# Two-layer hybrid decoder trunk: wide products of two weight parts for both blocks, then the narrow ones, in runs of sixteen

## The chip, the cores and the metric

The kernel runs on one NeuronCore of a Trainium2 chip. The time is device time of one execution, in microseconds (us). Several runs were timed, and one further execution was profiled; the profile gives the start and length of every instruction on each engine: TensorE (PE, with the weight load PEld apart), VectorE (DVE), ScalarE (ACT), GpSimd (POOL), and SyncE (SP), which here only issues transfers.

## The reference

A sequence of 256 positions with 2048 features goes through two layers, each of which adds its branch to the stream, and a last RMSNorm. Both branches project the normalised input, attend, multiply by a SiLU gate and project back. Cut to what matters:

```python
for i in range(2):
    h = rmsnorm(x, norm_g[i])
    if i == 0:      # forgetting attention, 32 heads of 64
        q, k, v, gate, f = split(h @ fox_w_in[0])          # 4 x 2048 + 32 columns
        c = cumsum(log_sigmoid(f + fox_b_f[0]))            # per head
        y = softmax(q k^T / 8 + c[t] - c[s], causal) v
        x = x + (y * silu(gate)) @ fox_w_out[0]
    else:           # window of 128, 32 query heads on 4 key heads, sinks
        q, k, v, gate = split(h @ swa_w_in[0])             # 2 x 2048 + 2 x 256 columns
        q, k = partial_rope(q), partial_rope(k)
        y = softmax(q k^T / 8, band, with sink) v
        x = x + (y * silu(gate)) @ swa_w_out[0]
return rmsnorm(x, final_g)
```

## The kernel before

**Products.** Every projection is cut into units of 256 output columns (`Unit`), and each unit's 2048 input features into parts, four of 512 in most units (a part is four tiles of 128 features). Values are float32, multiplied in two halves: `load` brings a part from memory (a transfer that SP issues into one of four buffers `wraw`), ACT rounds it (L222, the high half) and DVE subtracts (L223, the low half), both into one of five buffers `w` (`WBUFS`). The activations, `xs` and `ys`, lie split in the same way. `block(u, p, c)` issues the products of part `p` of unit `u` for one block `c` of 128 output rows (0 or 1). It has two steps: **wide** products, in which the high half of the stationary tile meets both halves of the moving one (512 columns), and **narrow** ones, in which its low half meets the high half (256 columns). For a part of four tiles these are four wide and four narrow products. `block` issues the wide ones and returns `narrow`, which issues the narrow ones and, after a unit's last part, calls its consumer (`done`). A unit accumulates in two PSUM banks, of which there are two pairs (`acc`). Units with `halves=False` (the values of layer 0, two groups at a time, and the last output unit) don't divide in this way.

**The stream.** `stream` is the list of all (unit, part) in order: layer 0 by groups of four heads (`fox_units`: queries, keys, for odd groups the values of two, gate), its output units (`first_out`, whose first three are interleaved by part), layer 1 (`swa_units`: keys, values, then for each of eight groups queries and gate), and its output units (`last_out`). The loop at the end walks it. At each part it first asks for the part three further on (`fetch`, L1019), issues block 0 of this part and then block 1 of the part before, so that block 1 runs one part late. For units in `quiet` (layer 0 from its third group on, output units from the fourth on) the narrow products of block 0 come after the whole of block 1: wide 4, wide 4, narrow 4, narrow 4, runs of eight. For all others, layer 1 among them, they follow at once: runs of four.

**What sets the order around it.** TensorE's instructions keep the order in which they are written. All else of the attention hangs on a clock of ticks: a tick passes after every two products of a `halves` unit, eight in a part, 32 in a unit, and `after(n, fn)` runs `fn` n ticks later. When a unit's keys (layer 0) or queries (layer 1) are complete, their consumer sets the group's events by a table: scores of the first and second pair of heads (`ps_s`), transposes (`pt`, `pt_w`), product with the values (`psy`). In layer 0 (`FOX_DUE`) the scores are due 18 and 50 ticks after the keys, in layer 1 (`SWA_DUE`) 31 and 49 after the queries. On ACT and DVE the order is the program's, as the scheduler of the build leaves it: casts and subtractions of weights stand in one queue with copies out of PSUM (L295), exponentials (L337), scalings (L356, L359) and the steps below.

**Lines that the steps touch.** Keys of layer 0: L295 copies half of the accumulators, L577 adds the other, L578 scales, and L582, L583 (ACT) and L585, L586 (DVE) write the split keys `kk`. Queries of layer 1: L295, L838 add, L840 shuffle, L843, L844 rotary products, L876 sum, L369 (ACT) and L370 (DVE) the split queries. Softmax of layer 1: scores and bias L453, L392, L457, maxima L887 to L890, exponentials L337, L893, L357, L353, scalings L356 and L359, transposes `pt_w`, copies L475 and L477. Gate: L324, L325, L312 to L319.

Of the kernel before, what the change touches and what calls it, by code (L numbers as in the profile page):

```python
# [49 lines left out]
WBUFS = 5  # L50
# [7 lines left out]
def trunk(  # L58
# [19 lines left out]
    def mm(*args, **kw):  # L78
        tc.keep_in_program_order(nc.tensor.matmul(*args, **kw))  # L79
# [28 lines left out]
    def tick():  # L108
        clock[0] += 1
        for fn in due.pop(clock[0], ()):  # L110
            with tc.high_priority(HP):
                fn()
# [99 lines left out]
    def load(unit, p):  # L212
        src, off, _, _, s = unit.parts[p]
        n = unit.n
        ask(unit, p, nc.sync)
        raw = unit.raw[:, off : off + s, :]
        w = wpool.tile([P, 2048], F32R, tag="w", name="w")
        w = w[:, 0 : 2 * s * n].rearrange("p (k h n) -> p k h n", h=2, n=n)
        high, low = w[:, :, 0, :], w[:, :, 1, :]
        if isinstance(src, tuple):  # L220
            high, low = (a.rearrange("p k (g n) -> p k g n", g=2) for a in (high, low))
        state["split"] = nc.scalar.copy(high, raw)  # L222
        nc.vector.tensor_tensor(out=low, in0=raw, in1=high.bitcast(F32), op=ALU.subtract)  # L223
        loaded[unit, p] = w

    def block(unit, p, c):
        _, _, _, kt0, s = unit.parts[p]
        w, a = loaded[unit, p], unit.acts
        if p == 0 and (c == 0 or unit.apart):

            pool, tag, banks = unit.apart if c == 1 else (*unit.acc, 2)
            ps = pool.tile([P, banks, 512], F32, tag=tag, name="acc")
            if unit.apart:
                unit.ps[c] = ps[:, 0, :]
            else:
                unit.ps, unit.both = [ps[:, i, :] for i in range(2)], ps
        n = unit.n if unit.kind == "tok" else S
        both, ps = unit.ps[c], unit.ps[c][:, 0:n]
        cs = slice(c * P, (c + 1) * P)
        def operands(i):  # L240

            kt = kt0 + i
            if unit.kind == "tok":
                return a[:, kt, 0, cs], a[:, kt, 1, cs], w[:, i]
            return w[:, i, 0, cs], w[:, i, 1, cs], a[:, kt]

        first, last = kt0 == 0, kt0 + s == KT
        ops = [operands(i) for i in range(s)]
        def done():
            if p < len(unit.parts) - 1:  # L250
                return
            if unit.apart:
                unit.consume(c, both)
            elif c == 1 and unit.kind == "tok":
                for i in range(2):
                    unit.consume(i, unit.ps[i])
            elif c == 1:
                unit.consume(unit.both)

        def narrow():  # L260
            for i, (_, sl, mv) in enumerate(ops):
                mm(ps, sl, mv[:, 0, :], start=False, stop=last and i == s - 1)
                if i % 2:
                    tick()
            done()

        if unit.halves:

            for i, (sh, _, mv) in enumerate(ops):
                mm(both, sh, mv.rearrange("p h n -> p (h n)"), start=first and i == 0, stop=False)  # L270
                if i % 2:
                    tick()
            if s % 2:
                tick()
            return narrow
        if n == 512:
            for i, (sh, sl, mv) in enumerate(ops):
                mm(ps, sh, mv[:, 0, :], start=first and i == 0, stop=False)
                mm(ps, sh, mv[:, 1, :], start=False, stop=False)
                tick()  # L280
                mm(ps, sl, mv[:, 0, :], start=False, stop=last and i == s - 1)
                tick()
        else:
            for i, (sh, sl, mv) in enumerate(ops):
                mm(ps, sh, mv[:, 0, :], start=first and i == 0, stop=False)
                mm(ps, sl, mv[:, 0, :], start=False, stop=False)
            for i, (sh, _, mv) in enumerate(ops):
                mm(ps, sh, mv[:, 1, :], start=False, stop=last and i == s - 1)
                tick()
        done()  # L290
        return lambda: None
# [13 lines left out]
    def whole(src, kind, consume, **kw):  # L305
        return Unit(quarters(src), kind, consume, **kw)
# [351 lines left out]
    groups = [FoxGroup(g) for g in range(8)]  # L658
# [36 lines left out]
    def out_units(src, done):  # L695
        def consumer(u):
            def consume(ps):
                x = xT[:, 2 * u : 2 * u + 2, :]
                nc.vector.tensor_add(x, low_half(ps), x)  # L699
                nc.vector.tensor_add(x, ps[:, :, 0:S], x)  # L700
                for c in range(2):
                    done(2 * u + c)

            return consume

        first = [
            whole(src[u], "wgt", consumer(u), acts=ys, acc=(ps_s, "S") if u == 2 else None)
            for u in range(3)
        ]
        return first + [whole(src[u], "wgt", consumer(u), acts=ys) for u in range(3, 8)]  # L710
# [115 lines left out]
    fox_units = units  # L826
    first_out = out_units(fox_out_d, to_layer1)
# [80 lines left out]
    swa_units = [whole(swa_in_d[8], "wgt", swa_k), whole(swa_in_d[9], "tok", swa_v)]  # L908
# [6 lines left out]
    last_out = out_units(swa_out_d, to_end)  # L915
# [56 lines left out]
    def fetch(upto):  # L972
        while fetched[0] < min(upto, len(stream)):
            load(*stream[fetched[0]])
            fetched[0] += 1
# [37 lines left out]
    state["sink"] = sink  # L1013

    quiet = set(fox_units[fox_units.index(groups[2].units[0]):] + first_out[3:] + last_out[3:7])
    prev = None
    for i, (u, p) in enumerate(stream):  # L1019
        fetch(i + 1 + LOOK)  # L1020
        if u is last_out[7]:
            if p == 0:
                block(*prev, 1)()
            block(u, p, 0)()
            continue
        narrow = block(u, p, 0)
        if u not in quiet:
            narrow()
        if prev is not None:
            block(*prev, 1)()  # L1030
        if u in quiet:
            narrow()
        prev = (u, p)
    for p in range(len(last_out[7].parts)):
        block(last_out[7], p, 1)()
# [65 lines left out]
```

## Time and profile before

| | us |
|---|---|
| median of 3 runs (825.01 to 825.56) | 825.55 |
| the profiled execution | 824.71 |
| its span, first to last instruction | 823.0 |
| mean granted TensorE clock | 0.996 |
| transfers, mean | 183 GB/s |

The page has the busy time of each engine (with the share of the span and the number of instructions), the chain of work that ended last, the costliest groups of instructions, and the transfers. Views of the trace list waits, groups and instructions by time. In rows of the timeline stand start, length, engine, line, operation, what it writes and reads, and how many; in brackets the idle time ahead of it and what ended it. Matmuls are pipelined and are recorded for longer than they hold the engine, so two starts tell more of them than a length.

### The profile page before, as it was taken

The numbers are of one execution on the slowest core, as the hardware profiler recorded it, in microseconds if no ns is written. First come the engines' busy times: TensorE is split into PE (matmuls) and PEld (weight loads), VectorE is DVE, ScalarE is ACT, GpSimd is POOL, SyncE is SP. The second block draws the span as 40 slices with busy tenths as digits, with TensorE's granted clock in tenths as the row PEclk, the third lists the DMA queues.
The fourth block names the chain that finished last, engine by engine and source line by source line (L and its number), as shares of the span: only waits on it lengthen the run. The fifth ranks groups of instructions, "written<-read, shape, count | busy, mean of one in ns | idle before, by whom it ended". The sixth has DMA issues, their size and how long they took to land.

```text
span 823.0 us, 13160 instructions
## 1 busy us (share of the span) xinstructions
PE 812.7 (99%) x4746; PEld 706.5 (86%) x4746; DVE 643.8 (78%) x1171; ACT 527.2 (64%) x978; POOL 63.5 (8%) x96
## 2 busy tenths in 40 slices
PE   8999999999999999999999999999999999999996
PEld 7988888888888888888888888888888888888885
DVE  6988866987678876788749668689999899976654
ACT  7776665665657566575647546577678776875551
POOL 1012010000101010010003110000000000001210
PEclk9999999999999999999999999999999999999998
DMA  9766656655656466655555565555455554464642
GB/s 294 252 213 225 195 186 199 198 176 178 208 167 218 153 195 202 192 196 162 175 181 187 187 203 162 187 165 180 141 164 161 175 170 139 154 195 146 206 126 102
DMA packets 47264, 150.49 MB, mean 183 GB/s; under 512 B 5552, under 2 KB 7248, under 8 KB 47200
## 3 DMA queue, kind: packets, MB, share of 16 engines
q1 hardware_dynamic: 44640, 141.84, 54.8%
q0 software_dynamic: 1408, 6.36, 2.3%
q10 hardware_dynamic: 1152, 1.47, 0.5%
q8 instruction: 37, 0.61, 0.3%
q14 instruction: 27, 0.22, 0.1%
HBM read 147.50 MB, written 2.15 MB: 182 GB/s over the span
## 4 chain that ended last, share of the span: by engine, by line
PE 98%; DMA 0%; DVE 0%; ACT 0%; DVEq 0%; issue 0%; SPq 0%
PE acc L79 90%; PE ps_s L79 3%; PE psy L79 3%; PE pt L82 1%; PE pt_w L82 1%; DMA wraw<-in_vf_dram 0%; DVE scaled L813 0%; PE ps_n L79 0%; PE rows L79 0%; DVEq L1095 0%; ACT w L222 0%; DVE tail_x L784 0%; PE pt_r L82 0%; DVE rest L788 0%; SPq L930 0%
## 5 line engine op out<-in xcount | busy, mean ns | idle before, releaser
L79 PE MATMUL acc<-xs,w 128*128 128x512 f32 (+1 forms) x2624 | 480.3, 339 | 0.0
L79 PEld LDWEIGHTS acc<-xs,w 128*128 128x128 f32 x2624 | 406.2, 189 | 56.7 <-issue 1.3
L223 DVE TENSOR_TENSOR w<-wraw,w 128x1024 fp32r<-128x1024 f32 (+4 forms) x277 | 324.8, 1178 | 92.2 <-ACT w L222 90.7
L222 ACT CAST w<-wraw 128x1024 fp32r<-128x1024 f32 (+4 forms) x277 | 277.7, 1009 | 125.1 <-PE acc L79 93.9
L79 PE MATMUL acc<-ys,w 128*128 128x256 f32 (+1 forms) x960 | 170.5, 338 | 0.0
L79 PEld LDWEIGHTS acc<-ys,w 128*128 128x128 f32 x960 | 147.8, 189 | 21.0 <-issue 0.6
L79 PE MATMUL acc<-w,xs 128*128 128x512 f32 (+2 forms) x512 | 111.9, 363 | 1.4 <-ACT w L222 1.3
L79 PEld LDWEIGHTS acc<-w,xs 128*128 128x128 f32 x512 | 86.0, 188 | 15.3 <-ACT w L222 1.5
L295 ACT COPY half<-acc 128x512 f32<-128x512 f32 x56 | 32.8, 586 | 78.7 <-PE acc L79 78.4
L337 ACT ACTIVATE st<-st,mx 128x128 f32<-128x128 f32 (+1 forms) x128 | 56.6, 443 | 2.1 <-DVE mx L641 2.1
L720 POOL TENSOR_TENSOR acc<-acc,sq 128x256 f32<-128x256 f32 x28 | 24.4, 871 | 88.1 <-ACT sq L714 87.0
L79 PE MATMUL ps_s<-kk,q 128*128 128x256 f32 (+1 forms) x160 | 30.4, 304 | 0.0
L392 DVE CUSTOM_DVE_ANT_0 st<-ps_s,st 128x128 f32<-128x128 f32 (+1 forms) x96 | 28.2, 332 | 0.9
L123 POOL TENSOR_SCALAR_AFFINE_SELECT bc<-bc 128x256 f32<-128x256 f32 x32 | 23.7, 759 | 64.2 <-DMA bc<-negc_d 64.2
L79 PEld LDWEIGHTS ps_s<-kk,q 128*128 128x128 f32 x160 | 24.5, 188 | 2.9 <-issue 0.2
L718 POOL COPY acc<-sq 128x256 f32<-128x256 f32 x2 | 1.4, 676 | 326.1 <-ACT sq L714 326.1
L519 ACT CAST ys<-gt 128x512 fp32r<-128x512 f32 x16 | 9.9, 619 | 25.1 <-DVE gt L518 25.1
L426 ACT COPY pts<-pt 128x384 f32<-128x384 f32 x32 | 15.3, 478 | 16.2 <-PE pt L82 16.2
L628 POOL DMA_DIRECT2D bc<-negc_d x16 | 8.9, 555 | 217.3 <-DVE mx L392 192.3
L337 ACT ACTIVATION_READ_ACCUMULATOR st<-st,mx 128x1 f32 x128 | 23.9, 187 | 0.0
L157 DVE SCALAR_TENSOR_TENSOR xs<-xT,g_sb,xs 128x256 fp32r<-128x256 f32 x32 | 20.6, 679 | 2.9 <-ACT xs L156 2.9
L699 DVE TENSOR_TENSOR xT<-half,xT 128x512 f32<-128x512 f32 x15 | 11.4, 758 | 12.3 <-ACT half L295 12.3
(146 smaller groups left out, 594.0 us busy)
## 6 DMA issues: line engine op xcount, KB each, us to landing
wraw<-in_fox_in_dram SPq DMA_DIRECT2D x96, 512.0 KB, 4.4
wraw<-in_swa_in_dram SPq DMA_DIRECT2D x72, 512.0 KB, 4.2
wraw<-in_fox_out_dram SPq DMA_DIRECT2D x32, 512.0 KB, 4.4
wraw<-in_swa_out_dram SPq DMA_DIRECT2D x32, 512.0 KB, 4.3
wraw<-in_fox_in_dram SPq DMA_DIRECT2D x54, 256.0 KB, 3.7
bc<-negc_d POOLq DMA_DIRECT2D x16, 384.0 KB, 4.7
wraw<-in_vf_dram SPq DMA_DIRECT2D x4, 288.0 KB, 4.7
xT<-in_xt_dram SPq DMA_DIRECT2D x2, 512.0 KB, 7.9
```

The lines of the kernel that those rows point to most:

```text
L79: tc.keep_in_program_order(nc.tensor.matmul(*args, **kw))
L82: tc.keep_in_program_order(nc.tensor.transpose(out, in_, ident))
L123: return nc.gpsimd.affine_select(out=ap, in_=ap, compare_op=ALU.is_ge, fill=NEG, base=base, pattern=pattern, channel_multiplier=mult,)
L157: nc.vector.scalar_tensor_tensor(out=xs[:, kt, 1, :], in0=xT[:, kt, :], scalar=g, in1=xs[:, kt, 0, :].bitcast(F32), op0=ALU.mult, op1=ALU. ...
L222: state["split"] = nc.scalar.copy(high, raw)
L223: nc.vector.tensor_tensor(out=low, in0=raw, in1=high.bitcast(F32), op=ALU.subtract)
L295: nc.scalar.copy(s, ps[:, :, S : 2 * S])
L337: nc.scalar.activation(st[:, hh, rng], st[:, hh, rng], AF.Exp, bias=nm[:, qb, hh : hh + 1], accum_out=l[:, qb, hh : hh + 1],)
L392: nc.vector.tensor_tensor_reduce(out=st, in0=high, in1=st, scale=self.scale, scalar=LOWEST, op0=ALU.add, op1=ALU.max, accum_out=self.mx[:, ...
L426: nc.scalar.copy(group.new_pts(self.j, hh)[:, hh, self.j, :], pt[:, 0 : 3 * P])
L699: nc.vector.tensor_add(x, low_half(ps), x)
L720: nc.gpsimd.tensor_add(sums[0], sums[0], s)
```

## The change

The set `quiet` becomes `paired` and takes in the units of layer 1. Units in it that divide into wide and narrow go through a path of their own: at an even part the next five parts are asked for, then the wide products of both blocks are issued, and their narrow ones are held; at the odd part the wide products of both blocks follow, and then all narrow ones: wide 16, narrow 16. The next part is asked for once the even part's narrow products are issued. Block 1 no longer runs a part late there, and a unit's consumer comes at the unit's own end. All other units keep the order of before.

```diff
-    quiet = set(fox_units[fox_units.index(groups[2].units[0]):] + first_out[3:] + last_out[3:7])
-    prev = None
+    paired = fox_units[fox_units.index(groups[2].units[0]):] + first_out[3:] + last_out[3:7]
+    paired += swa_units
+    paired = {u for u in paired if u.halves}
+    prev, held = None, []
     for i, (u, p) in enumerate(stream):
+        if u in paired:
+            if p % 2 == 0:
+                if prev is not None:
+                    block(*prev, 1)()
+                    prev = None
+                fetch(i + WBUFS)
+            held += [block(u, p, c) for c in range(2)]
+            if p % 2:
+                for k, narrow in enumerate(held):
+                    narrow()
+                    if k == 1:
+                        fetch(i + WBUFS)
+                held = []
+            continue
         fetch(i + 1 + LOOK)
         if u is last_out[7]:
-            if p == 0:
+            if p == 0 and prev is not None:
                 block(*prev, 1)()
             block(u, p, 0)()
             continue
-        narrow = block(u, p, 0)
-        if u not in quiet:
-            narrow()
+        block(u, p, 0)()
         if prev is not None:
             block(*prev, 1)()
-        if u in quiet:
-            narrow()
         prev = (u, p)
```

Counted over TensorE's whole order, a narrow product is followed by a wide one 364 times before and 196 times now. The number of products is the same.

**DVE, keys of layer 0, group 6** (groups 2 and 4 alike). `w` is a subtraction of weights. Before:

```order
L223 TENSOR_TENSOR w<-wraw,w 128x4x256 x3
L577 TENSOR_TENSOR k<-acc,half 128x512
L578 TENSOR_TENSOR k<-k,r_n_497 128x512
L223 TENSOR_TENSOR w<-wraw,w 128x4x256
L585 TENSOR_TENSOR kk<-k,kk 64x2x256
```

Now:

```order
L223 TENSOR_TENSOR w<-wraw,w 128x4x256 x3
L577 TENSOR_TENSOR k<-acc,half 128x512
L223 TENSOR_TENSOR w<-wraw,w 128x4x256
L578 TENSOR_TENSOR k<-k,r_n_497 128x512
L585 TENSOR_TENSOR kk<-k,kk 64x2x256
```

A subtraction moved ahead of L578, and the last of the three ahead of L577 is of a part whose buffer comes free only at the eighth narrow product of the keys' last pair.

**ACT, layer 1, the end of a group's second pair of heads.** `es` is the sinks' exponential, `pts` the transposed weights, `half` the copy of the next group's queries. Before:

```order
L891 ACTIVATE es<-es 128x4
L337 ACTIVATE st,l<-st,mx 128x128
L337 ACTIVATE st,l<-st,mx 128x256
L475 COPY pts<-pt_w 128x2x128
L295 COPY half<-acc 128x512
L356 ACTIVATE st<-st,rl 128x128 x2
L359 ACTIVATE st<-st,rl 128x128 x2
L222 CAST w<-wraw 128x4x256 x2
```

Now:

```order
L891 ACTIVATE es<-es 128x4
L337 ACTIVATE st,l<-st,mx 128x128
L337 ACTIVATE st,l<-st,mx 128x256
L222 CAST w<-wraw 128x4x256
L356 ACTIVATE st<-st,rl 128x128 x2
L359 ACTIVATE st<-st,rl 128x128 x2
L295 COPY half<-acc 128x512
L222 CAST w<-wraw 128x4x256 x2
```

The copy of the queries stands behind a cast and the four scalings.

**DVE, layer 1, the queries that follow.** `rot_t` and `rot` are the rotated queries. Before:

```order
L838 TENSOR_TENSOR rot_t<-acc,half 128x512
L840 STREAM_SHUFFLE rot<-rot_t 128x512
L843 TENSOR_TENSOR rot_t<-rot_t,rope_c 128x512
L844 TENSOR_TENSOR rot<-rot,rope_c 128x512
L223 TENSOR_TENSOR w<-wraw,w 128x4x256
L477 TENSOR_TENSOR pts<-pt_w,apart 128x2x256
L876 TENSOR_TENSOR rot_t<-rot_t,rot 128x512
L223 TENSOR_TENSOR w<-wraw,w 128x4x256
L370 TENSOR_TENSOR q_5495<-rot_t,q_5495 64x2x256 x2
```

Now:

```order
L838 TENSOR_TENSOR rot_t<-acc,half 128x512
L840 STREAM_SHUFFLE rot<-rot_t 128x512
L223 TENSOR_TENSOR w<-wraw,w 128x4x256
L477 TENSOR_TENSOR pts<-pt_w,apart 128x2x256
L843 TENSOR_TENSOR rot_t<-rot_t,rope_c 128x512
L844 TENSOR_TENSOR rot<-rot,rope_c 128x512
L223 TENSOR_TENSOR w<-wraw,w 128x4x256
L876 TENSOR_TENSOR rot_t<-rot_t,rot 128x512
L223 TENSOR_TENSOR w<-wraw,w 128x4x256
L370 TENSOR_TENSOR q_5486<-rot_t,q_5486 64x2x256 x2
```

Three subtractions instead of two lie between the sum L838 and the split queries.

## The prediction

> **What bounds the kernel now.** I read the page's busy line and its chain first, then the windows by stage.
>
> ```profile
> PE 812.7 (99%) x4746; PEld 706.5 (86%) x4746; DVE 643.8 (78%) x1171; ACT 527.2 (64%) x978; POOL 63.5 (8%) x96
> PE 98%; DMA 0%; DVE 0%; ACT 0%; DVEq 0%; issue 0%; SPq 0%
> L79 PE MATMUL acc<-xs,w 128*128 128x256 f32 x1312 | 206.9, 283 | 0.0
> 498.00:745.00 247.00, 247.00 (x1464) 213.25 (x1464) 213.62 (x462) 175.36 (x385) 0.00 (x0) 1.00 0.53 167
> wraw<-in_swa_in_dram SPq DMA_DIRECT2D x72, 512.0 KB, 4.2
> ```
>
> 98% of the chain that ends last is TensorE, so the time is the sum of what its products take; nothing else delays it. But the fourth row, the stretch of layer 1's input products (columns: stretch, length, then busy PE, PE weight load, DVE, ACT, POOL, clock), has DVE busy for 213.62 of 247 us and ACT for 175.36. Both are close behind, and in the trace both work through their instructions in the program's order. (The third row is used below: a narrow product is recorded for 0.28 us, so its result is there 0.16 after the next one may start.) Two numbers matter therefore: what TensorE saves by the regrouping, and whether the two queues still deliver the operands of the score products in time.
>
> **What the longer runs save.** Two rows of the chain cover 182 products each; the four after them, of the timeline, are runs of one width alone.
>
> ```profile
> 213.07 31.44 PE acc L79 x182
> 505.82 31.97 PE acc L79 x182
> 284.64 3.56 PE L79 MATMUL acc<-w,xs 128*128 128x512 f32 x15
> 288.04 0.40 PE L79 MATMUL ps_s<-kk,q 128*128 128x256 f32 x2
> 802.10 5.92 PE L79 MATMUL acc<-w,ys 128*128 128x256 f32 x48
> 807.86 0.50 PE L79 MATMUL ps_cols<-ones,acc 128*128 128x1 f32 x4
> ```
>
> From start to start, a wide product in a long run takes (288.04 - 284.64) / 15 = 0.2267 us and a narrow one (807.86 - 802.10) / 48 = 0.1200. The first chain row lies where runs are of eight: by the program's order it holds 88 wide and 94 narrow products, 19.95 + 11.28 = 31.23 us at those rates, so 0.21 us remain for 11 returns from narrow to wide, **0.019 us each**. The second, in runs of four, holds 92 and 90: 31.66 us, and 0.31 remain for some 22 returns, 0.014 each. The change takes 28 units from four returns to two (28 x 2 x 0.019 = 1.06 us), and 18 units of layer 1 from eight to two (18 x (8 x 0.014 - 2 x 0.019) = 1.33). That is **2.4 us less**. No trace here has runs of sixteen: if a return there cost nothing, the saving would be 28 x 4 x 0.019 + 18 x 8 x 0.014 = 4.1; if it cost twice as much, 4.1 - 92 x 0.038 = 0.6. I take the cost of a run of eight, the nearest row. The number of products, of ticks and of loads does not change.
>
> [...]
>
> **Loads.** A wide run now uses two parts, so a buffer of split weights comes free after 8 of the 16 narrow products and the next at their end, about 0.95 and then 4.6 us apart instead of every 2.8. SP issues the same transfers, whose landing (4.2 us, row above) stays ahead because the raw tiles have four buffers; each part is still asked for two pairs, some 8 to 11 us, before its first product, and needs two passes of 1.05 and 1.2 us. I cost this at nothing for TensorE. Its effect is on the queues: a cast that waits for such a buffer holds what stands behind it on ACT.
>
> **Layer 0, the keys of groups 2, 4 and 6.** These rows are of group 6; DVE first, then ACT, then PE.
>
> ```profile
> 334.25 1.22 DVE L223 TENSOR_TENSOR w<-wraw,w 128x1024 fp32r<-128x1024 f32 x1 [1.57 <-ACT w L222]
> 336.53 0.69 DVE L577 TENSOR_TENSOR k<-acc,half 128x512 f32<-128x512 f32 x1 [1.06 <-ACT half L295]
> 337.25 0.69 DVE L578 TENSOR_TENSOR k<-k,r_n 128x512 f32<-128x512 f32 x1
> 339.00 0.68 DVE L585 TENSOR_TENSOR kk<-k,kk 64x512 fp32r<-64x512 f32 x1
> 341.11 0.69 DVE L586 TENSOR_TENSOR kk<-k,kk 64x512 fp32r<-64x512 f32 x1
> 335.91 0.59 ACT L295 COPY half<-acc 128x512 f32<-128x512 f32 x1 [1.70 <-PE acc L79]
> 337.98 0.62 ACT L582 CAST kk<-k 64x512 fp32r<-64x512 f32 x1 [0.54 <-DVE k L578]
> 341.77 0.63 PE L79 MATMUL ps_s<-kk,q 128*128 128x512 f32 x2
> ```
>
> The last key half is ready at 341.11 + 0.69 = 341.80 and the second score product starts at about 342.0: 0.2 us to spare, on a chain of 5.9 us from the end of the unit at 335.9. In the new order the end of the unit moves to its own sixteenth narrow product, and TensorE comes to the scores after a whole pair (16 x 0.2267 + 0.02 = 3.65, and 16 x 0.12 = 1.92, together 5.57) and four wide products (0.93): the second score product is due 6.73 after the unit's last issue. The keys, with the same zero: a weight subtraction (1.22) now stands ahead of L577 and starts only at 0.33, since its cast waited for the eighth narrow product and DVE for the cast; L577 ends at 2.16; another 1.15 of subtraction now stands between L577 and L578, which ends at 3.90; the cast L582 and the four alternating passes L585, L586 take 3.5 as now (337.94 to 341.80 is 3.86, less a subtraction's hold of the first); end 7.4. **TensorE waits 7.4 - 6.7 = 0.7 us, three times: 2.1.** Bounds 0.4 to 1.0 each, by half a subtraction either way.
>
> **Layer 1, the queries of every odd group.** ACT, then DVE, then PE, around an even group's second pair and the next group's queries.
>
> ```profile
> 594.06 1.05 ACT L222 CAST w<-wraw 128x1024 fp32r<-128x1024 f32 x1 [1.32 <-issue]
> 595.01 0.40 ACT L337 ACTIVATE st<-st,mx 128x128 f32<-128x128 f32 x1
> 596.88 0.62 ACT L312 ACTIVATE gate_e<-gt 128x512 f32<-128x512 f32 x1
> 602.17 0.39 ACT L337 ACTIVATE st<-st,mx 128x128 f32<-128x128 f32 x1
> 604.09 0.35 ACT L475 COPY pts<-pt_w 128x256 f32<-128x256 f32 x1
> 604.34 0.58 ACT L295 COPY half<-acc 128x512 f32<-128x512 f32 x1
> 604.89 0.70 ACT L356 ACTIVATE st<-st,rl 128x128 f32<-128x128 f32 x2
> 606.08 1.04 ACT L222 CAST w<-wraw 128x1024 fp32r<-128x1024 f32 x1
> 600.83 0.69 DVE L315 SCALAR_TENSOR_TENSOR gate_e<-gt,gate_e 128x512 f32<-128x512 f32 x1
> 605.29 0.68 DVE L838 TENSOR_TENSOR rot_t<-acc,half 128x512 f32<-128x512 f32 x1
> 606.79 0.69 DVE L843 TENSOR_TENSOR rot_t<-rot_t,rope_c 128x512 f32<-128x512 f32 x1
> 608.00 1.22 DVE L223 TENSOR_TENSOR w<-wraw,w 128x1024 fp32r<-128x1024 f32 x1
> 609.14 0.68 DVE L477 TENSOR_TENSOR pts<-pt_w,apart 128x512 f32<-128x512 f32 x1
> 609.74 0.68 DVE L876 TENSOR_TENSOR rot_t<-rot_t,rot 128x512 f32<-128x512 f32 x1
> 611.58 1.40 DVE L370 TENSOR_TENSOR q<-rot_t,q 64x512 fp32r<-64x512 f32 x2
> 607.58 0.60 PE L82 MATMUL pt_w<-ident,st 128*128 128x128 f32 x4
> 607.93 7.01 PE L79 MATMUL acc<-xs,w 128*128 128x512 f32 x38
> 614.78 0.88 PE L79 MATMUL ps_s<-kk,q 128*128 128x256 f32 x6
> ```
>
> Now the queries are ready at 612.98 and the scores start at 614.78: 1.8 us to spare. In the new order, from the end of an even group's first score products (zero): a cast ahead of the first exponentials waits for the eighth narrow product of the next pair, 0.24 + 3.65 + 0.95 + 0.16 = 5.0, and takes 1.05. The exponentials (1.87, 595.01 to 596.88) end near 8.0. DVE then does the sums of the first pair (0.6), the rest of the second pair's reductions (0.9), L315 (0.65), one subtraction (1.2) and two small ones: 11.45. The second exponentials (1.92) end at 13.8, and a cast (0.95) and the four scalings (1.2) now stand **ahead** of the copy L295, which stood ahead of them: the copy ends at 16.4 though its products were done at 12.7. From there DVE runs without a gap: L838 0.7, the shuffle 0.75, subtraction 1.15, L477 0.6, L843 and L844 1.25, subtraction 1.15, L876 0.65, subtraction 1.15, twice L370 1.4: 8.8, one subtraction more than now, **end 25.2**. TensorE: the query unit ends at 0.24 + 5.57 + two wide 0.47 + six score products 0.71 + 14 wide 3.2 + six narrow 0.71 + transposes 0.35 + ten narrow 1.28 = 12.5; then 3.65 + 0.95 wide and narrow, 0.35 of transposes, 1.05, 3.65 and 14 narrow ones 1.68, and the second score product is due at 23.95. **It waits 1.25 us at groups 1, 3, 5, 7: 5.0.** Bounds 0.75 to 1.75, by half a subtraction on a chain of 20 steps. At the even groups the scores' place moves behind the values' products, which last 2.8 us; I get 26.85 against 26.95 and take no wait. The first transposes of an even group come 0.24 after their scalings: none.
>
> At the outputs of both layers the regrouping makes the attention's last events come 2 to 4 ticks earlier against the stream, up to 1.4 us more room for the last quarter of `ys`; this only hides better and is worth nothing.
>
> **Sum.** -2.4 + 2.1 + 5.0 = +4.7 us. The profiled execution took 824.71 us (span 823.0), so 829.4 there; the median of the runs, 825.55, is 0.84 above it, which gives **830.2**.
>
> **Rivals.** (1) The queues keep up and only the saving is left: 825.55 - 2.4 = 823.15, faster. Place: the two score waits. It decides if the query chain is 1.25 us (one subtraction) and the key chain 0.7 shorter than I walked, or if the waits of casts release earlier. For it speaks that every step was hidden before; against it, that both key and query chains gain whole subtractions in front of them in the program's order. Chance 0.17. (2) One of the two waits is real and the other not, most simply the keys' alone: 825.55 - 2.4 + 2.1 = 825.25, no change. Chance 0.14. (3) The remainder per return is no price of the order and comes back in the long runs: saving 0, waits whole, 825.55 + 7.1 = 832.65. That both rows show a remainder speaks against it; chance 0.11. [...]
>
> **How the numbers follow.** The forecast has 0.58. Its own range, by the bounds of the waits (1.2 to 3.0 and 3.0 to 7.0) and of the saving, mixed, is 827 to 833. A measurement of this kernel tells about 0.2% (1.65 us) from no change. Slower: forecast and (3), 0.69; same: (2), 0.14; faster: (1), 0.17. To leave out no more than 0.2 the range goes down into (1) and holds all of (2): 823.0 to 833.2.
>
> **What would show it.** Right: 32 products of a pair in 5.57 us; in the list of waits a TensorE idle ahead of score products (`ps_s`) released by DVE, from L586 three times at 0.7 and L370 four times at 1.25; DVE and ACT busy times unchanged. Wrong: no such waits, or waits ahead of the transposes or of `acc` instead, from casts.

## The result and the profile after

The median is **832.34 us** (832.11 to 832.51, five runs) against 825.55 of the kernel before (824.68 to 826.44, five runs beside it): a ratio of 1.0084, interval 1.0073 to 1.0096. The change makes the kernel slower by 6.8 us. The profiled execution took 832.51 us, its span 830.8, at a granted clock of 0.997. The forecast was 830.2, for two waits; both are there, and a third that it did not name.

Two lines of the page of the changed kernel, busy times and the chain that ended last:

```profile
PE 814.8 (98%) x4746; PEld 708.8 (85%) x4746; DVE 630.9 (76%) x1171; ACT 528.3 (64%) x978; POOL 57.8 (7%) x96
PE 87%; DVE 6%; ACT 3%; issue 3%; DMA 0%; POOL 0%; DVEq 0%; SPq 0%
```

The stretch of layer 1's input products in the same kernel's view by windows (columns as in the prediction's fourth row):

```profile
498.00:745.00 247.00, 243.17 (x1441) 210.97 (x1440) 208.77 (x459) 177.21 (x386) 1.52 (x2) 1.00 0.52 163
```

The chain was 98% TensorE and is 87% now: it leaves TensorE and runs back through DVE and ACT. In the stretch of 247 us TensorE, which was busy without a gap, now stands idle for 247.00 - 243.17 = 3.83 us, while DVE and ACT have about the work that they had (208.77 and 177.21 us, where it was 213.62 and 175.36). Which products wait, and for what, is in the view of TensorE's waits (total us, times, longest):

```profile
PE ps_s L79 <- DVE q L370: 3.0, 8, 0.5
PE ps_s L79 <- DVE kk L586: 2.0, 3, 0.7
PE ps_n L79 <- POOL acc L720: 0.8, 1, 0.8
```

The view of the kernel before has none of the three. It counts idle time between recorded ends, and a matmul's record is longer than it holds the engine (a narrow product is recorded for 0.284 us on the mean in this kernel, and the next starts 0.120 after it), so the loss is read from starts. **Keys**: the timeline of the changed kernel, group 6, DVE, then ACT, then PE.

```profile
337.82 1.23 DVE L223 TENSOR_TENSOR w<-wraw,w 128x1024 fp32r<-128x1024 f32 x1 [2.85 <-ACT w L222]
338.97 0.68 DVE L577 TENSOR_TENSOR k<-acc,half 128x512 f32<-128x512 f32 x1
339.57 1.22 DVE L223 TENSOR_TENSOR w<-wraw,w 128x1024 fp32r<-128x1024 f32 x1
340.70 0.69 DVE L578 TENSOR_TENSOR k<-k,r_n 128x512 f32<-128x512 f32 x1
...
344.19 0.69 DVE L586 TENSOR_TENSOR kk<-k,kk 64x512 fp32r<-64x512 f32 x1
336.75 1.05 ACT L222 CAST w<-wraw 128x1024 fp32r<-128x1024 f32 x1 [3.22 <-issue]
337.70 0.58 ACT L295 COPY half<-acc 128x512 f32<-128x512 f32 x1
343.96 0.40 PE L79 MATMUL ps_s<-kk,q 128*128 128x512 f32 x1
345.02 0.47 PE L79 MATMUL ps_s<-kk,q 128*128 128x512 f32 x1 [0.67 <-DVE kk L586]
```

The copy of the keys is done at 338.28, but DVE is in a subtraction until 338.97, and a second one holds L578 for 1.13 us more. The last key half ends at 344.88; the second score product, due 0.23 after the first, at 344.19, starts at 345.02. That is 0.83 us, and the same in groups 2 and 4: 2.5 us together.

**Queries**: the same kind of rows around group 3.

```profile
608.18 1.04 ACT L222 CAST w<-wraw 128x1024 fp32r<-128x1024 f32 x1
609.12 0.70 ACT L356 ACTIVATE st<-st,rl 128x128 f32<-128x128 f32 x2
609.71 0.69 ACT L359 ACTIVATE st<-st,rl 128x128 f32<-128x128 f32 x2
610.30 0.57 ACT L295 COPY half<-acc 128x512 f32<-128x512 f32 x1
610.91 0.69 DVE L838 TENSOR_TENSOR rot_t<-acc,half 128x512 f32<-128x512 f32 x1 [0.43 <-ACT half L295]
612.27 1.21 DVE L223 TENSOR_TENSOR w<-wraw,w 128x1024 fp32r<-128x1024 f32 x1
615.19 1.22 DVE L223 TENSOR_TENSOR w<-wraw,w 128x1024 fp32r<-128x1024 f32 x1
616.93 1.22 DVE L223 TENSOR_TENSOR w<-wraw,w 128x1024 fp32r<-128x1024 f32 x1
618.18 1.40 DVE L370 TENSOR_TENSOR q<-rot_t,q 64x512 fp32r<-64x512 f32 x2
619.01 0.36 PE L79 MATMUL ps_s<-kk,q 128*128 128x256 f32 x1 [0.49 <-DVE q L370]
619.64 0.39 PE L79 MATMUL ps_s<-kk,q 128*128 128x256 f32 x1 [0.27 <-DVE q L370]
```

The copy stands behind a cast and four scalings, three subtractions follow between L838 and L370, and TensorE waits ahead of both halves. Against six undisturbed starts, 0.12 apart, the six score products lose 1.26 us here and in groups 1, 5 and 7: 5.0 us. In the even groups they lose 0.07, 0.2 together.

**The norm of layer 1**, not forecast: the chain of the changed kernel, followed back from its first product.

```profile
495.14 0.69 DVE xT L699
495.82 1.18 DVE w L223
497.00 0.61 DVE xT L700
...
498.05 0.41 ACT sq L714
...
499.35 0.80 POOL acc L720
500.15 0.04 issue
```

When the last output unit of layer 0 is done, DVE adds it to the stream (L699, L700), ACT squares it, POOL adds the squares, and `after(16, norm)` lets TensorE sum them 16 ticks later. Now a subtraction stands between L699 and L700, and one ahead of L699 had waited for the unit's eighth narrow product, as at the keys. From start to start TensorE loses 1.05 us.

Put together: 2.5 + 5.0 + 0.2 + 1.05 = 8.75 us of waits. The medians differ by 6.8, so the longer runs save about 2.

### The profile page after: what moved, and what is told of

It reads as the page before. It is cut to its first block, busy times and chain, and to the rows that moved or that the text cites. A ratio compares the mean times of both kernels' runs of the same rounds, so it can differ in the third digit from the quotient of the medians.

```text
span 830.8 us, 13144 instructions
## 1 busy us (share of the span) xinstructions
PE 814.8 (98%) x4746; PEld 708.8 (85%) x4746; DVE 630.9 (76%) x1171; ACT 528.3 (64%) x978; POOL 57.8 (7%) x96
## 4 chain that ended last, share of the span: by engine, by line
PE 87%; DVE 6%; ACT 3%; issue 3%; DMA 0%; POOL 0%; DVEq 0%; SPq 0%
PE acc L79 79%; PE ps_s L79 3%; PE psy L79 3%; DVE w L223 2%; PE pt L82 1%; ACT w L222 1%; ACT st L337 1%; PE pt_w L82 1%; DVE kk L585 0%; DVE kk L586 0%; DMA wraw<-in_vf_dram 0%; DVE q L370 0%; DVE rot_t L838 0%; DVE rot_t L876 0%; DVE rot L844 0%
## 5 line engine op out<-in xcount | busy, mean ns | idle before, releaser
L79 PE MATMUL acc<-ys,w 128*128 128x512 f32 (+1 forms) x960 | 169.5, 338 | 0.0
L79 PE MATMUL ps_s<-kk,q 128*128 128x256 f32 (+1 forms) x160 | 32.7, 311 | 5.1 <-DVE q L370 3.0
L79 PEld LDWEIGHTS ps_s<-kk,q 128*128 128x128 f32 x160 | 24.8, 188 | 10.5 <-issue 3.4
L123 POOL TENSOR_SCALAR_AFFINE_SELECT bc<-bc 128x256 f32<-128x256 f32 x32 | 18.7, 606 | 67.2 <-DMA bc<-negc_d 67.2
L156 ACT ACTIVATE xs<-xT,g_sb 128x256 fp32r<-128x256 f32 x32 | 15.4, 501 | 12.5 <-DVE xT L700 11.8
L157 DVE SCALAR_TENSOR_TENSOR xs<-xT,g_sb,xs 128x256 fp32r<-128x256 f32 x32 | 16.8, 547 | 7.1 <-ACT xs L156 7.1
L369 ACT CAST q<-rot_t 64x512 fp32r<-64x512 f32 x16 | 9.9, 618 | 18.9 <-DVE rot_t L876 18.7
```

Of the source, the lines that this page charges most:

```text
L123: return nc.gpsimd.affine_select(out=ap, in_=ap, compare_op=ALU.is_ge, fill=NEG, base=base, pattern=pattern, channel_multiplier=mult,)
L156: nc.scalar.activation(xs[:, kt, 0, :], xT[:, kt, :], AF.Copy, scale=g)
L157: nc.vector.scalar_tensor_tensor(out=xs[:, kt, 1, :], in0=xT[:, kt, :], scalar=g, in1=xs[:, kt, 0, :].bitcast(F32), op0=ALU.mult, op1=ALU. ...
```

## The experiments

Runs of the kernel before beside the first four had a median of 825.31 us, beside the next four 825.26, beside the last 825.39.

**1. Layer 0 and the outputs alone.** Layer 1 keeps its runs of four.

```diff
-    paired += swa_units
```

> Layer 0 and the output units in runs of sixteen, layer 1 in runs of four as before. Theory A (the loss is TensorE waiting for the split keys and queries, 0.83 us at three key halves and 1.26 at four query halves): only the key waits are left, 825.55 - 28 x 0.04 + 2.5 = 826.9. Theory B (the runs of sixteen are themselves slow, spread over all 46 units): 28 of 46 units, 825.55 + 6.8 x 28 / 46 = 829.7.

Measured: 827.95 us (827.65 to 828.59, seven runs), ratio 1.0029, interval 1.0018 to 1.0040. The three waits of 0.83 us are there, those of the queries are gone, and the wait ahead of the norm stays, since the last output unit is still paired: 2.5 + 1.0 against a difference of 2.6, which leaves a saving of 0.9.

**2. Layer 1's input units alone.** All other units keep the order of before.

```diff
+    quiet = set(fox_units[fox_units.index(groups[2].units[0]):] + first_out[3:] + last_out[3:7])
+    paired = {u for u in swa_units if u.halves}
```

> Layer 1 alone in runs of sixteen, everything else as before. Theory A: four query waits of 1.26 and three of 0.07, less 18 units x 0.07: 825.55 + 5.25 - 1.3 = 829.5, and 830.5 if the wait ahead of layer 1's norm (0.95 with what follows) comes with it. Theory B: 825.55 + 6.8 x 18 / 46 = 828.2, without TensorE idle ahead of score products.

Measured: 829.47 us (828.67 to 830.07, four runs), ratio 1.0045, interval 1.0029 to 1.0062. The query waits are there in full, the keys' and the norm's are not: 5.2 against 4.2, a saving of 1.0. (Its profiled execution also waited 0.9 us ahead of `ps_s`, for DVE, at 73.8 us. That far the instructions are those of the kernel before, whose profile has no such wait; the profiled execution took 830.07 us, 0.6 more than the median.) The two halves add up to the whole, so layer 0's waits have nothing to do with layer 1's.

**3. Priority for the consumers of keys and queries.** The scheduler of the build is told to put their steps first.

```diff
+            elif c == 1 and unit in state.get("eager", ()):
+                with tc.high_priority(HP):
+                    unit.consume(unit.both)
...
+    state["eager"] = {G.units[1] for G in groups[1:]} | {swa_units[2 + 2 * k] for k in range(8)}
```

> The changed kernel, with the consumers of keys and queries at the priority of the ticks. In the program's order this moves the copy of the queries ahead of a cast and four scalings on ACT; the keys' order stays. If the queue order makes the query wait (theory A): the copy comes 2.1 us earlier, the four waits go, 832.3 - 5.0 = 827.3, key waits unchanged at 0.83. If the wait is set by when weight buffers come free (theory C): no gain, 832.3.

Measured: 826.74 us (826.22 to 827.57, ten runs), ratio 1.0017, interval 1.0008 to 1.0027. The timeline of this kernel, ACT, DVE, PE (its lines stand three lower than before: L298 is the copy, L359 and L362 the scalings):

```profile
605.77 0.57 ACT L298 COPY half<-acc 128x512 f32<-128x512 f32 x1
606.23 1.06 ACT L222 CAST w<-wraw 128x1024 fp32r<-128x1024 f32 x1
607.18 0.71 ACT L359 ACTIVATE st<-st,rl 128x128 f32<-128x128 f32 x2
607.78 0.69 ACT L362 ACTIVATE st<-st,rl 128x128 f32<-128x128 f32 x2
613.65 1.41 DVE L373 TENSOR_TENSOR q<-rot_t,q 64x512 fp32r<-64x512 f32 x2
615.96 0.28 PE L79 MATMUL ps_s<-kk,q 128*128 128x256 f32 x1
```

With the copy ahead of cast and scalings the queries are ready at 615.06, 0.9 us before their product. All the query waits are gone, and the time falls by 5.6, although three subtractions still lie between L838 and L370. So for the queries it was the copy's place that decided, and theory C, which expected no gain, falls for them. The keys' order on DVE did not change by the priority, and neither did their wait, as this kernel's list has it:

```profile
PE ps_s L79 <- DVE kk L589: 2.0, 3, 0.7
```

**4. Weights asked for one part later.**

```diff
-                fetch(i + WBUFS)
+                fetch(i + WBUFS - 1)
...
-                        fetch(i + WBUFS)
+                        fetch(i + WBUFS - 1)
```

> The changed kernel, each part asked for one place later, so that its buffer of split weights has been free for a whole wide run and no cast waits for TensorE. If casts that wait for a buffer hold the queues (theory C): both the key waits (0.83 to about 0.2) and the query waits (1.26 to 0.3 or less) shrink, 832.3 - 1.9 - 4.5 = 825.9. If only the number of subtractions in the chains counts: they stay as many, and the time stays near 832. If the lead is now too short: TensorE idle ahead of acc, released by casts.

Measured: 827.09 us (826.78 to 827.54, ten runs), ratio 1.0020, interval 1.0011 to 1.0030. The query waits are gone once more, those of the keys (0.83 us) and of the norm are not, and once more the copy stands behind the exponentials and ahead of cast and scalings. For the keys this run tells nothing: buffers go round in the order of the stream, so a part keeps its buffer however late it is asked for, and in the keys' stretch the order on ACT and DVE came out as in the changed kernel.

**5. More room for the waiting products.** No order of the weights is touched.

```diff
-FOX_DUE = ((18, 48), (50, 81), 110)
+FOX_DUE = ((22, 50), (52, 83), 112)
-SWA_DUE = ((31, 59), (49, 76), 87)
+SWA_DUE = ((35, 63), (53, 80), 91)
-            after(16, norm)
+            after(20, norm)
```

> The changed kernel with its order of weights and consumers untouched, but the events that TensorE waited at come four ticks (eight products) later: scores of layer 0's keys from its third group on at 22 instead of 18 (the rest of that table 2 later), scores of layer 1's queries at 35 instead of 31 (the rest 4 later), and the norm of layer 1 at 20 instead of 16. Theory A (the three waits are all that the change costs, 2.5 + 5.0 + 0.2 + 1.05 us, and the longer runs save some 2): every wait ahead of ps_s and of ps_n is gone, nothing takes its place, 823.6 us, below the kernel before. Rival B (the room is borrowed: what comes later pushes the values' products or the next group's scores into the same queues): waits reappear ahead of psy or the transposes, and the time stays at 827 to 832.

Measured: 829.33 us (829.27 to 829.70, five runs), ratio 1.0053, interval 1.0041 to 1.0066. The wait that this kernel's list has in their place:

```profile
PE pt L82 <- DVE st L348: 4.1, 4, 1.2
```

The first transposes of group 6 in its timeline:

```profile
358.30 0.70 PE L82 MATMUL pt<-ident,st 128*128 128x128 f32 x3 [0.98 <-DVE st L348]
```

The three waits are gone. In layer 1, where all events moved by four ticks, nothing took their place, as theory A has it. Rival B is right for layer 0: TensorE waits ahead of the transposes instead, four times (groups 2, 4, 6 and 7), 5.9 us from start to start. 832.34 - 8.75 + 5.9 = 829.5. Two things stand behind it. The scores were moved by four ticks and the transposes behind them by two, so the softmax between them had two ticks, four products, less. And with the due times the build's order on ACT changed, though the edit touches neither weights nor gate. The first two rows are of the changed kernel, the other two of this one:

```profile
353.66 0.49 ACT L337 ACTIVATE st<-st,mx 128x256 f32<-128x256 f32 x1
354.15 0.62 ACT L312 ACTIVATE gate_e<-gt 128x512 f32<-128x512 f32 x1
354.00 0.63 ACT L312 ACTIVATE gate_e<-gt 128x512 f32<-128x512 f32 x1 [1.81 <-DVE gt L325]
355.87 0.39 ACT L337 ACTIVATE st<-st,mx 128x128 f32<-128x128 f32 x1
```

Three steps of the gate (L312 to L314) now stand ahead of the four exponentials, where they stood behind the last of them, and it is the same in all four groups. How the 5.9 us divide between the two was not tried. A later due time lends room only to what moves with it, and it can change the order in the queues as well.

**6. Only the norm later.** `after(20, norm)` alone, the last two lines of the diff above.

> The changed kernel with one number changed: the norm of layer 1 comes 20 instead of 16 ticks after the last output unit of layer 0. Theory A (the wait ahead of ps_n, which I did not forecast, costs 1.05 us by itself): that wait is gone, all others stay, 831.3 us. Rival B (the products behind it would have waited for the norm's result anyway, so the time only moves): another wait of 1 us appears behind it, 832.3.

Measured: 831.23 us (830.92 to 831.53, four runs), ratio 1.0075, interval 1.0061 to 1.0089. The wait is gone, the others stay, 1.1 us less: nothing behind the norm took it up.

**7. The keys' chain freed of the two subtractions.** The two loads are asked for after the keys' last pass.

```diff
-                nc.vector.tensor_sub(kk[other, :, hh, 1, :], t[w], high)
+                state["kk"] = nc.vector.tensor_sub(kk[other, :, hh, 1, :], t[w], high)
...
+                if p == 0 and u in after_keys:
+                    with tc.issue_after(state["kk"].ins):
+                        fetch(i + WBUFS)
+                else:
+                    fetch(i + WBUFS)
...
-                    if k == 1:
+                    if k == 1 and (p < 3 or u not in keys):
```

> The changed kernel with one thing undone at layer 0's keys from the second group on: the two loads of weights that fall into the end of the key unit are asked for behind the keys' last pass, so that no subtraction stands between L577 and L578 and none that waits for the last pair stands ahead of L577; the scores stay where they are, at 18 ticks. Theory A (the two subtractions in front of the key chain make the wait): the key chain ends some 1.8 us earlier, the three waits of 0.83 us ahead of ps_s are gone at groups 2, 4 and 6, those of the queries and of the norm stay: 832.3 - 2.5 = 829.8. Rival B (the scores are simply due too early in the new order, whatever stands in the queue, because the second step of the keys' casts sets the end): 0.4 us or more of each wait stays: 831 or more. Rival C: the loads asked for later make TensorE wait for weights instead (acc released by w L223).

Measured: 831.13 us (830.27 to 831.56, five runs), ratio 1.0071, interval 1.0058 to 1.0084. The timeline of group 6:

```profile
341.12 0.69 DVE L586 TENSOR_TENSOR kk<-k,kk 64x512 fp32r<-64x512 f32 x1
341.84 2.36 DVE L223 TENSOR_TENSOR w<-wraw,w 128x1024 fp32r<-128x1024 f32 x2
342.55 0.62 PE L79 MATMUL ps_s<-kk,q 128*128 128x512 f32 x2
```

The keys are ready at 341.81, 0.97 us before the second score product is due at 342.78; in the changed kernel they were 0.69 late. So the two subtractions made the wait, and the due time of 18 ticks was enough without them: rival B falls. Rival C falls too, since TensorE's waits for weights in this run (three, 1.4 us together) all lie in the first 11 us. The gain is 1.2 us and not 2.5. From start to start some 1.4 us of short delays stand at other places of layer 0: 0.16 in each of three groups at the scores that follow ten ticks after those of the first pair, 0.46 and 0.42 at the transposes of groups 2 and 4. The subtractions that were put behind the keys now stand in front of other steps.

**8. All three at once.** Experiment 7, the priority of experiment 3 for the queries alone, and the norm at 20 ticks.

> The changed kernel with all three chains freed at once: the keys as in the run before this one, the queries' steps of layer 1 given priority as in the third experiment, the norm at 20 ticks. Theory A (waits 2.5 + 5.2 + 1.05 are all that the change cost, and what is left is the saving of the longer runs): 823.6 us, 0.2% faster than the kernel before; no wait ahead of ps_s or ps_n. Rival B (the saving is nothing, and the rest of the time is another cost): 825.3 or more.

Measured: 824.12 us (823.39 to 826.10, eleven runs), ratio **0.9989**, interval 0.9980 to 0.9998. All of its waits of TensorE:

```profile
PE rows L79 <- DVE tail L802: 2.3, 1, 2.3
PE acc L79 <- ACT w L222: 1.2, 1, 1.2
PE warm L79 <- DVE ones L116: 1.1, 1, 1.1
```

Its stretch of layer 1's input products:

```profile
498.00:745.00 247.00, 247.00 (x1472) 214.31 (x1471) 211.62 (x463) 178.47 (x386) 0.56 (x1) 1.00 0.52 168
```

No score and no norm waits, and in the window TensorE is busy for all of the 247 us. (The three that are left, at the two ends of the program, the changed kernel has as well.) The time is 8.2 us below the changed kernel and 1.1 below the one before, about 0.1%, less than the 0.2% that I took for measurable; the interval leaves 1 out by little. With 1.2 us of short delays that it keeps in layer 0 (from start to start), the saving of the longer runs is 825.26 - 824.12 + 1.2 = 2.3 us. Rival B, no saving, does not fit that.

**9. The price of a return by itself.** The kernel before, with every narrow product of layer 1's input units right behind its wide one.

```diff
+        if unit in state.get("mixed", ()):
+            for i, (sh, sl, mv) in enumerate(ops):
+                mm(both, sh, mv.rearrange("p h n -> p (h n)"), start=first and i == 0, stop=False)
+                mm(ps, sl, mv[:, 0, :], start=False, stop=last and i == s - 1)
+                tick()
+            done()
+            return lambda: None
...
+    state["mixed"] = set(swa_units)
```

> The kernel before with one thing changed, in the other direction: in layer 1's 18 input units each wide product is followed at once by its narrow one, so that a unit returns from narrow to wide 32 times instead of 8 (432 returns more in all); products, loads, ticks and events are as before. Theory A (a return has a price of its own, 0.014 to 0.019 us by the rows of before, whatever the length of the run): a wide and a narrow product together take 0.361 to 0.366 us from start to start instead of 0.347, and the time is 6.0 to 8.2 us above the kernel before, 831.3 to 833.5. Rival B (the time of a product depends on its width alone, as a gap by width has it): 0.347 us a pair, no change, 825.3. Rival C (the price belongs to the end of a run, and short runs cost less): between the two, under 4 us.

Measured: 826.10 us (825.90 to 826.76, ten runs), ratio 1.0008, interval 0.9998 to 1.0018. A piece of this kernel's chain, of 18 wide and 18 narrow products in turn:

```profile
592.04 6.35 PE acc L79 x36
```

A wide and a narrow product take 6.35 / 18 = 0.353 us together, against 0.2267 + 0.1200 = 0.3467 in long runs: a return costs 0.006 here. Theory A falls as a rule for all lengths: 432 more returns cost 0.7 us, not 6 to 8. The interval of the time does not exclude rival B, no change, but the 0.353 does. Of the three, rival C comes nearest: a return costs 0.006 us after runs of one, against the 0.014 after runs of four.

## Why the prediction was right in its waits, and where it was off

| term | forecast | measured |
|---|---|---|
| longer runs | -2.4 | -2.1 |
| keys of layer 0, three times | 0.7 each, 2.1 | 0.83 each, 2.5 |
| queries of layer 1, four times | 1.25 each, 5.0 | 1.26 each, 5.0 |
| even groups of layer 1 | 0 | 0.07 each, 0.2 |
| norm of layer 1 | not named | 1.05 |
| sum | +4.7 | +6.65 |

The medians differ by 6.8. Of the 2.1 us by which the forecast was too low, the norm makes 1.05, the keys 0.4, the longer runs 0.3 and the even groups 0.2.

**Queries.** Here the walk through the queues held step by step. With the end of the even group's first scores (594.52) as zero, the copy was to end at 16.4 and ended at 16.35 (610.30 + 0.57); the queries were to be ready at 25.2 and were at 25.06 (618.18 + 1.40). Experiments 3 and 4 show that the step I set in bold, cast and scalings ahead of the copy, decides: without it the wait goes. The third subtraction, which I counted too, has room without it.

**Keys.** Mechanism and place as forecast, and experiment 7 shows the cause. The end was to come 7.4 us after the unit's last issue. The unit's last issue lies 6.73 ahead of the second score product's due time, 344.19 - 6.73 = 337.46, and the keys were ready at 344.88: 7.42. I rounded 7.4 - 6.7, and left out what the wait costs beyond the operand's end: the product starts 0.14 after it (345.02). That is the 0.1 us of each.

**The norm.** This is the step that failed. I wrote of the outputs that the regrouping "only hides better and is worth nothing", and had looked there at the attention's last events alone. The end of the last output unit is an end of a unit like the keys', with a chain that DVE, ACT and POOL share; there the same two subtractions move in front, and its product is due 16 ticks later. In the kernel before, its last squares were added by 496.71, and `ps_n` came at 497.35:

```profile
495.03 1.68 POOL L720 TENSOR_TENSOR acc<-acc,sq 128x256 f32<-128x256 f32 x2 [9.99 <-ACT sq L714]
497.35 0.59 PE L79 MATMUL ps_n<-acc,ones 128*128 128x256 f32 x2
```

So 0.64 us were to spare there, which two rows would have told. Experiment 6 shows its price alone: 1.1 us, half of what the forecast lacked.

**The longer runs.** The rates were right: an undisturbed pair of parts takes 5.567 us (median of 46 such pairs, from start to start), where I had 5.57. By them 2.4 us would be saved. The medians of experiments 1, 2 and 8 give 0.9 + 1.0 and 2.3, but the intervals of the first two leave 0.9 and 1.4 us either way. The traces tell it closer. Take every two projection products in a row, subtract 0.2267 or 0.1200 from the time between their starts, and sum from the product on where the orders part (at 117.0 us in the kernel before): 9.9 us remain in the kernel before and 7.7 in the changed one, so 2.1 are saved, 1.35 in layer 1 (forecast 1.33) and 0.8 in layer 0 and the outputs (forecast 1.06). In the same way experiment 1 saves 0.7, experiment 2 1.3 and experiment 8 2.3. So this term was 0.3 too large, and why layer 0 saves less than its count of returns stays open. Rival 3, a saving of 0, came nearer to the time (832.65) than the forecast did, and is wrong all the same: with the waits removed the kernel is 1.1 us faster than before (experiment 8), where a saving of 0 would leave it as it was.

**Rivals 1 and 2** said that one or both waits stay hidden; both were there. Loads cost TensorE nothing more, as forecast: the list of waits has one wait for a cast of weights, 1.2 us, where the kernel before has one of 1.3.

## What to carry to other kernels

Regrouping products to save 2 us moved every "end of a unit" against the casts and subtractions that share ACT's and DVE's queues; so list every chain that starts at such an end (here keys, queries and the norm), and for each write down its spare time and what now stands in front of it. A wait that comes from the order in a queue went away by another order (experiments 3, 7 and 8), which can put the displaced steps in front of others (1.4 us in experiment 7). It also went away by a later due time where all that follows moved as far or nothing stood close behind (layer 1 in experiment 5, the norm in experiment 6); where the next event moved by less, and the queue's order changed with it, a longer wait came (layer 0 in experiment 5). And when the total comes out near a rival's number, the ledger of waits has to say whether it is that rival.

## What the runs showed of the hardware that was not expected

**Runs of one width.** Over all undisturbed runs in three traces, a run of N wide and N narrow products takes longer than N x 0.3467 us by 0.006 us at N = 1 (508 runs, experiment 9), 0.014 at 4 (139, the kernel before), 0.020 at 8 (78, the same) and 0.020 at 16 (46, the changed kernel). In runs of eight and sixteen the extra lies in the first five wide products: from start to start 233, 236, 228, 232 and 231 ns, then 227 to the end of the run, while the first narrow product behind them takes 113 and the rest 120. So these runs do not show one price of a switch, which would be the same at every length: the extra grows over the first products of a run, from 0.006 us at one to 0.020 at eight, and is no larger at sixteen. Nor does the width alone set the time of a product: the place in the run matters as well, 228 to 236 ns against 227 for a wide one and 113 against 120 for a narrow one. Why the first five are slower stays open.

**The start.** The two profiled executions differ by 7.8 us in span, the medians by 6.8. Their programs are the same up to 117 us, yet the first norm came 1.2 us later in the second: at 34.22 us in the kernel before and at 35.41 in the changed one.

```profile
35.41 0.59 PE L79 MATMUL ps_n<-ssq,ones 128*128 128x256 f32 x2
```

All of that arises ahead of 15 us: the 41st projection product starts at 13.01 us in the one and at 14.21 in the other. Up to 10.4 us a wide product of the changed kernel's execution takes 0.427 us from start to start and a narrow one 0.213; in that of the kernel before most take 0.23 and 0.12 from 6.4 us on. The view by windows gives 1.00 as the clock from 5 to 10 us in both, but the traces' entries of the clock begin only at 4.0 us in the one and at 10.5 in the other, so the reason is not shown. In the trace of experiment 8 the first norm came at 35.50, in an execution that was faster than the median of before. So one execution's span varies by as much as one of the waits that are discussed here, and the waits were priced by starts within a trace and not by differences of spans. Counted from the product where the orders part to the last projection product, the kernel before takes 697.1 us, the changed one 704.1 and that of experiment 8 696.2.
